# Two constants of the scheduler's cost table, set while a two-layer hybrid trunk is built

## The chip, the cores and the metric

The kernel runs on one core of one Trainium2 chip. The metric is the time of one execution on the device in microseconds (us), taken from before the first instruction to after the last. The core has a matrix engine (TensorE, PE in the rows), a vector engine (VectorE, DVE), a scalar engine (ScalarE, ACT), GpSimd (POOL), a queue that issues the transfers (SyncE, SP) and 16 DMA engines. Each engine works through its own list of instructions in the order in which the program has them, and waits on semaphores for the others.

## What is computed

Two layers of a decoder trunk for 512 positions and a width of 1024, batch 1. Each layer normalises its input, projects it once, sends the pieces through three causal mixers (A: a state-space block in chunks, "SSD"; B: a diagonal complex scan, "S5"; C: attention with low-rank queries and keys, "MLA"), gates and sums the three, and projects back:

```python
for l in range(DEPTH):                       # DEPTH = 2
    h = rms_norm(x, pre_norm[l])
    proj = h @ w_in[l]
    z_a, xbc, dt_raw, u_b, z_b, c_q, c_kv, k_rope, z_c, gate_logits = split_columns(proj)
    y_a = ssd_branch(z_a, xbc, dt_raw, ...) @ w_a[l]
    y_b = s5_branch(u_b, z_b, ...) @ w_b[l]
    y_c = mla_branch(c_q, c_kv, k_rope, z_c, ...) @ w_c[l]
    gates = sigmoid(gate_logits).reshape(bsz, s, N_BRANCH, D_MODEL)
    merged = gates[..., 0, :] * y_a + gates[..., 1, :] * y_b + gates[..., 2, :] * y_c
    out = merged @ w_o[l]
    x = x + rms_norm(out, post_norm[l])
```

## The kernel before

Everything is float32. TensorE multiplies in a rounded float32, so each operand is split into a high part and the rest, and a product is made of three matmuls: high by high, high by low, low by high. `mm3` (L61, L62, L63) does that for small products. `dense` does it for a block of 128 output rows by 512 positions with 1024 inputs: sixteen matmuls with the high weights (L116 and L117, by turns with the activation's high and low part), then eight with the low weights (L119).

A weight block comes through `weight`: one transfer of 512 KB on SP's queue into `wf` (L102; L100 where the block is gathered from eight pieces in DRAM), a cast on ScalarE into `wh` (L66), and a subtraction on VectorE or GpSimd into `wl` (L78, L81). Each of the three tiles has two buffers, so a load waits until the block two before has been split. The results stand in PSUM: three banks `mm` for dense blocks, three banks `aux` for small products, and the two tags `pM` and `pb` (tiles `pM`, `pm`, `pk`, `pr`).

One layer goes through these stages (times of the first layer; the second repeats them some 980 us later):

- 0 to 50 us: normalising, and the first two projections.
- 50 to 380 us: attention (`mla`) for four groups of heads, and between its steps, by `fill`, the pieces of `s5_prep`, which build the S5 filters: transposes into `pm` (L377), `pmh` and `pml` split from it, small products `pM` (L386, L387) and `pk` (L395), and results stored in DRAM as `kpad` and `odr`.
- 380 to 490 us: the S5 scan over 63 steps (`s5_scan`, L896 to L899, four small VectorE operations a step on the tile `ms`, 252 in all), beside the eight merges of branch C on TensorE.
- 490 to 690 us: SSD. Convolutions on VectorE (`keep`, L69) behind dense projections; for each of four groups the product `aux` of the split tiles `bfh`, `bfl` and `cfh`, `cfl` (L61 to L63), and small products after it.
- 690 to 840 us: eight S5 blocks (`s5_block`): each loads `uf`, `sf`, `kpad` (eight pieces of 64 KB) and `odr`, splits them, and multiplies (`pM`); its result `ys` is transposed into an `aux` bank (L936). Each block stands beside a dense projection and a merge of branch A.
- 840 to 1030 us: the GLU, the merges of branch B, and the output projection.

The order of each engine's list is not written by hand. The program is recorded step by step, and while it is recorded a scheduler inside `tile.TileContext(nc, schedule_with_timeline_sim=True)` (L1228) puts the instructions in order: it plays the program through with a table of costs and, at each point of its own clock, takes for each engine an instruction whose inputs it holds to be ready. Buffers are handed out in the order of the program's text, so the dependencies are the same whatever the order. Two entries of the table matter here: the gap that it adds to every matmul at full clock (2.5 ns), and the delay between the end of a transfer and the moment at which a waiting engine sees it (900 ns).

The names in the rows and orders are those of the tiles; a number behind a name is the buffer.

## Time and profile before

| | us |
|---|---|
| time, median of 3 runs | 1972.35 (1971.62 to 1976.9) |
| profiled execution | 1977.92 |
| its span, first to last instruction | 1976.1 |
| TensorE busy | 1870.3 (95%) |
| VectorE busy | 1420.3 (72%) |
| ScalarE busy | 914.2 (46%) |
| GpSimd busy | 631.9 (32%) |
| TensorE's granted clock, mean | 0.967 of full speed |

The profile is of one execution. Its own time lies 1.8 us above its span, and 5.6 us above the median of the runs; a difference is worked out within it and then put on the median. Busy time of an engine counts an instruction from its start to its end. Matmuls overlap, so TensorE counts as busy from the start of one to the end of the next. An idle time stands in brackets behind the instruction that ended it, with the one that released it.

### The profile page before, as it was taken

Reading aid. Unit: us, or ns where it says so; the run is one execution under the profiler, and the core shown is the slowest. Engines: PE = TensorE matmul, PEld = TensorE weight load, DVE = VectorE, ACT = ScalarE, POOL = GpSimd, SP = SyncE. Lnnn points to the kernel's source line nnn. Section 1 sums busy time; section 2 is a strip of 40 time slices with the busy share of each in tenths; the row PEclk is TensorE's granted clock in tenths of the full one; section 3 lists DMA queues with packets and bytes.
Section 4 is the critical chain, followed back from the end, with each engine's and each line's share of the span. In section 5 each row is a group of like instructions: output and inputs, shape, how many; then the busy total and the mean of one; then the engine's idle time right before and its main releaser. Section 6 shows DMA issues by size and latency. Waiting matters only on the chain.

```text
span 1976.1 us, 28153 instructions
## 1 busy us (share of the span) xinstructions
PE 1870.3 (95%) x9880; PEld 1528.1 (77%) x9880; DVE 1420.3 (72%) x2882; ACT 914.2 (46%) x1647; POOL 631.9 (32%) x679
## 2 busy tenths in 40 slices
PE   7898999899999989999998989999999999999998
PEld 5687777687877868888876877776878887788887
DVE  6866566799999857744578566667999996776443
ACT  4355455522555545533332555554235663554331
POOL 1746656201233201201118465661013331012010
PEclk9898998899999999999997999998999999999999
DMA  5343333322321266345233334343332224662541
GB/s 158 94 114 94 108 114 103 119 92 84 128 65 64 75 187 182 92 152 167 90 83 90 111 93 122 100 128 96 96 130 75 74 76 113 183 174 86 171 128 43
DMA packets 136253, 219.99 MB, mean 111 GB/s; under 512 B 39856, under 2 KB 79408, under 8 KB 135600
## 3 DMA queue, kind: packets, MB, share of 16 engines
q1 hardware_dynamic: 136112, 218.19, 37.1%
q8 instruction: 78, 1.28, 0.3%
q14 instruction: 63, 0.52, 0.1%
HBM read 182.08 MB, written 31.33 MB: 108 GB/s over the span
## 4 chain that ended last, share of the span: by engine, by line
PE 60%; DVE 22%; DMA 9%; ACT 3%; issue 2%; POOL 2%; SPq 2%; DVEq 0%; ACTq 0%; POOLq 0%
PE mm L116 15%; PE mm L117 14%; PE mm L119 14%; DMA wf<-in_w_in 3%; DVE wl L78 3%; DVE keep L69 3%; PE mm L61 2%; PE mm L62 2%; PE mm L63 2%; PE aux L61 1%; DVE tmp L69 1%; DVE ms L899 1%; PE aux L62 1%; PE aux L63 1%; DVE sc_t L896 1%
## 5 line engine op out<-in xcount | busy, mean ns | idle before, releaser
L116 PE MATMUL mm<-hh,wh 128*128 128x512 f32 (+1 forms) x1232 | 499.5, 405 | 11.5 <-ACT wh L66 8.0
L66 ACT ACTIVATE wh<-wf 128x1024 fp32r<-128x1024 f32 (+1 forms) x294 | 291.3, 994 | 440.2 <-PE mm L117 227.2
L117 PE MATMUL mm<-hl,wh 128*128 128x512 f32 (+1 forms) x1232 | 492.0, 399 | 0.0
L78 DVE TENSOR_TENSOR wl<-wf,wh 128x1024 fp32r<-128x1024 f32 (+1 forms) x243 | 294.8, 1218 | 188.1 <-ACT wh L66 154.3
L119 PE MATMUL mm<-hh,wl 128*128 128x512 f32 (+1 forms) x1232 | 314.9, 393 | 1.9 <-DVE wl L78 1.9
L116 PEld LDWEIGHTS mm<-hh,wh 128*128 128x128 f32 (+1 forms) x1232 | 236.5, 192 | 72.2 <-ACT wh L66 11.6
L117 PEld LDWEIGHTS mm<-hl,wh 128*128 128x128 f32 (+1 forms) x1232 | 236.2, 192 | 48.5 <-issue 0.5
L119 PEld LDWEIGHTS mm<-hh,wl 128*128 128x128 f32 (+1 forms) x1232 | 228.2, 188 | 52.6 <-DVE wl L78 2.3
L81 POOL TENSOR_TENSOR mg<-mg,tmp 128x512 f32<-128x512 f32 x32 | 77.7, 2431 | 458.1 <-DVE tmp L78 240.5
L81 POOL TENSOR_TENSOR wl<-wf,wh 128x1024 fp32r<-128x1024 f32 (+1 forms) x51 | 108.9, 2135 | 302.6 <-PE mm L119 209.3
L116 PE MATMUL mm<-ah,wh 128*128 128x512 f32 x512 | 200.3, 393 | 0.0
L117 PE MATMUL mm<-al,wh 128*128 128x512 f32 x512 | 199.9, 391 | 0.0
L119 PE MATMUL mm<-ah,wl 128*128 128x512 f32 x512 | 127.6, 390 | 0.0
L116 PEld LDWEIGHTS mm<-ah,wh 128*128 128x128 f32 x512 | 96.2, 188 | 21.4 <-ACT pkf L66 0.7
L117 PEld LDWEIGHTS mm<-al,wh 128*128 128x128 f32 x512 | 96.1, 188 | 20.9 <-issue 1.0
L119 PEld LDWEIGHTS mm<-ah,wl 128*128 128x128 f32 x512 | 95.7, 188 | 19.6
L617 DVE CUSTOM_DVE_ANT_0 sc<-aux,cmask 128x128 f32<-128x128 f32 (+3 forms) x128 | 60.9, 485 | 63.5 <-PE aux L63 62.5
L66 ACT ACTIVATE sc<-sc,nm 128x128 f32<-128x128 f32 (+3 forms) x128 | 70.4, 554 | 13.3 <-DVE nm L73 13.2
L81 POOL TENSOR_TENSOR pv<-pq,ar 128x288 f32<-128x288 f32 x64 | 49.1, 789 | 77.2 <-PE pk L395 68.7
L69 DVE SCALAR_TENSOR_TENSOR keep<-mm,cw,keep 128x511 f32<-128x511 f32 (+2 forms) x96 | 71.1, 740 | 2.0 <-ACT keep L66 1.5
L66 ACT ACTIVATE tmp<-mm 128x512 f32<-128x512 f32 x76 | 44.8, 592 | 56.2 <-PE mm L63 31.5
L81 POOL TENSOR_TENSOR pw<-pbb,ar 128x256 f32<-128x256 f32 x64 | 51.0, 799 | 41.8 <-PE pm L377 41.6
(346 smaller groups left out, 4002.8 us busy)
## 6 DMA issues: line engine op xcount, KB each, us to landing
wf<-in_w_in SPq DMA_DIRECT2D x156, 512.0 KB, 3.6
odr<-pv SPq DMA_DIRECT2D x64, 128.0 KB, 2.0
wf<-in_w_c SPq DMA_DIRECT2D x16, 512.0 KB, 3.4
wf<-in_w_a SPq DMA_DIRECT2D x16, 512.0 KB
wf<-kpad SPq DMA_DIRECT2D x128, 64.0 KB, 6.4
wf<-odr SPq DMA_DIRECT2D x16, 512.0 KB, 7.1
wf<-in_w_glu SPq DMA_DIRECT2D x16, 512.0 KB, 3.4
wf<-in_w_b SPq DMA_DIRECT2D x16, 512.0 KB, 3.8
```

What stands on the lines that cost most here:

```text
L61: mm(out, ah, bh, start=start, stop=False)
L62: mm(out, ah, bl, start=False, stop=False)
L63: mm(out, al, bh, start=False, stop=stop)
L66: self.nc.scalar.activation(out, in_, func, **kw)
L69: self.nc.vector.scalar_tensor_tensor(out, in0, s, in1, op0, op1)
L78: self.nc.vector.tensor_tensor(out, a, b, op)
L81: self.nc.gpsimd.tensor_tensor(out, a, b, op)
L116: mm(ps[:m], wh[:, o(i)], bh, start=i == 0, stop=False)
L117: mm(ps[:m], wh[:, o(i)], bl, start=False, stop=False)
L119: mm(ps[:m], wl[:, o(i)], bh, start=False, stop=i == k - 1)
L617: nc.vector.tensor_tensor_reduce(out=sc, in0=ps[:, :n], in1=self.cmask[:, 512 - n:512], op0=ALU.add, op1=ALU.max, scale=1.0, scalar=-3.0e3 ...
L896: nc.vector.tensor_tensor(t1, sc1, s, ALU.mult)
```

## The change

The function `measured_costs` sets two entries of the scheduler's cost table while the program is built, and puts the old values back afterwards. The gap of a matmul at full clock goes from 2.5 ns to 13.6 ns, the delay behind a transfer from 900 ns to 1600 ns. The text of the trunk is the same.

```diff
@@ -1,4 +1,4 @@
-from contextlib import ExitStack
+from contextlib import ExitStack, contextmanager
 
 import numpy as np
 
@@ -1214,6 +1214,22 @@
     return d
 
 
+@contextmanager
+def measured_costs():
+
+    from concourse.hw_specs import TRN2Spec
+
+    costs = {"PE_FULL_CLOCK_PASS_GAP_NS": 13.6, "SEM_PROP_DMA_OVERHEAD_NS": 1600}
+    saved = {k: getattr(TRN2Spec, k) for k in costs}
+    for k, v in costs.items():
+        setattr(TRN2Spec, k, v)
+    try:
+        yield
+    finally:
+        for k, v in saved.items():
+            setattr(TRN2Spec, k, v)
+
+
 def kernel(**inputs):
     import concourse.bacc as bacc
     from concourse.bass_utils import run_bass_kernel_spmd
@@ -1225,7 +1241,7 @@
         for n, v in arrays.items()
     }
     out = nc.dram_tensor("out_0", (T, D), F32, kind="ExternalOutput").ap()
-    with tile.TileContext(nc, schedule_with_timeline_sim=True) as tc:
+    with measured_costs(), tile.TileContext(nc, schedule_with_timeline_sim=True) as tc:
         trunk(tc, aps, out)
     r = run_bass_kernel_spmd(nc, [{f"in_{n}": v for n, v in arrays.items()}], core_ids=[0])
     return r.results[0]["out_0"].reshape(1, T, D)
```

The two programs hold the same instructions on every engine, 9714 on TensorE, 2874 on VectorE, 1489 on ScalarE, 684 on GpSimd and 1041 on SP, with the same buffers. What differs is the order of each list. It is the same from 0 to 50 us, through most of 745 to 1000 us, from 1400 to 1440 us and from 1725 us to the end. It differs in the attention stages, at the end of each scan, in SSD, and in the first S5 blocks. Three places follow; a line with - is where an instruction stood, one with + where it stands now.

**Place A**, the end of the scan in layer one. First VectorE's list around `wl_5309`, the low weights of a projection, and `keep_5260`, a convolution; `ms_4355` and `sc_t` belong to the scan.

```order
 L69 SCALAR_TENSOR_TENSOR keep_5221<-tmp_5226,keep_5221 128x512
 L78 TENSOR_TENSOR wl_5309<-wf_5307,wh_5308 128x1024
-L898 TENSOR_TENSOR ms_4355<-ms_4355,sc_t1_4357 128x64
 L69 SCALAR_TENSOR_TENSOR keep_5260<-mm_5235,cw_5177,keep_5260 128x511
-L899 TENSOR_TENSOR ms_4355<-ms_4355,sc_t2_4358 128x64
 L69 SCALAR_TENSOR_TENSOR keep_5260<-mm_5235,cw_5177,keep_5260 128x510
-L896 TENSOR_TENSOR sc_t1_4357<-sc1_0_560,ms_4355 128x64
-L897 TENSOR_TENSOR sc_t2_4358<-sc2_0_561,ms_4355 128x64
 L69 SCALAR_TENSOR_TENSOR keep_5260<-mm_5235,cw_5177,keep_5260 128x509
```

The scan's operations that stood among these stand ahead of them now: 238 of the 252 stood ahead of `wl_5309`, now all 252. Ahead of the last step of `keep_5260` it is 252 in place of 246.

TensorE's list behind this: `mm_5375` is a dense projection, `aux_5354` the first product of SSD, of the tiles `cf` (split from `keep_5260`) and `bf` (split from `keep_5221`).

```order
 L117 MATMUL mm_5375<-hl_111,wh_5370 128x512
 L116 MATMUL mm_5375<-hh_110,wh_5370 128x512
+L61 MATMUL aux_5354<-cfh_5348,bfh_5346 128x128
 L117 MATMUL mm_5375<-hl_111,wh_5370 128x512
 L116 MATMUL mm_5375<-hh_110,wh_5370 128x512
 L117 MATMUL mm_5375<-hl_111,wh_5370 128x512
+L62 MATMUL aux_5354<-cfl_5349,bfh_5346 128x128
+L63 MATMUL aux_5354<-cfh_5348,bfl_5347 128x128
```

The twelve matmuls of `aux_5354` stood 45 dense matmuls later; VectorE's `cfl_5349`, which they read, has moved forward as well, past the last convolution steps of `keep_5299`, those of `keep_5338`, and a block of low weights. In layer two the same place has 244 scan operations ahead of `wl_15093` where 232 stood.

**Place B**, the third and fourth S5 block of layer one. ScalarE's list: `wh_7650` and `wh_7851` are cast from the `odr` of two blocks, a block apart, `wh_7742` and `wh_7792` from dense weights, `ys` and `gl` belong to the blocks' results.

```order
 L66 ACTIVATE wh_7650<-wf_7649 128x1024
-L66 ACTIVATE wh_7792<-wf_7791 128x1024
-L66 ACTIVATE tmp_7739<-mm_7714 128x512
+L66 ACTIVATE wh_7742<-wf_7741 128x1024
+L66 ACTIVATE keep_7621<-mm_7596 128x512
 L66 ACTIVATE gl_7583<-aux_7574 128x512
 L66 ACTIVATE ys_7655<-pM_7656 64x4x8x16
@@ -608,9 +605,11 @@
 L66 ACTIVATE ys_7655<-pM_7657 64x4x8x16
 L66 ACTIVATE wh_7851<-wf_7850 128x1024
+L66 ACTIVATE wh_7792<-wf_7791 128x1024
```

The cast `wh_7792` stood behind `wh_7650` and stands behind `wh_7851`; `wh_7742` and `wh_7709` ahead of it have also moved back by a block. On SP's queue the loads of these weights have moved behind the pieces of `kpad` and the `odr` of their block, which they stood ahead of.

TensorE's list in the same place: `mm_7714` and `mm_7747` are dense blocks, `pM_7656` is the product of the third S5 block, and `wh_7637` is split from its `kpad`.

```order
 L116 MATMUL mm_7714<-hh_110,wh_7709 128x512
 L117 MATMUL mm_7714<-hl_111,wh_7709 128x512
-L119 MATMUL mm_7714<-hh_110,wl_7710 128x512 x8
-L116 MATMUL mm_7747<-ah_5755,wh_7742 128x512
-L117 MATMUL mm_7747<-al_5756,wh_7742 128x512
-L116 MATMUL mm_7747<-ah_5808,wh_7742 128x512
-L117 MATMUL mm_7747<-al_5809,wh_7742 128x512
-L116 MATMUL mm_7747<-ah_6224,wh_7742 128x512
-L117 MATMUL mm_7747<-al_6225,wh_7742 128x512
 L61 MATMUL pM_7656<-wh_7637,uh_7626 64x128
```

The eight matmuls with `wl_7710` and six of `mm_7747` that stood ahead of `pM_7656` have gone behind it, and four more follow. Further on, the transposes `aux_7775` of the block's result have moved ahead of the sixteen matmuls of `mm_7797` with `wh_7792`. In SSD the product of each of the three later groups (`aux_5821`, `aux_6290`, `aux_6759`, as `aux_5354` above) has likewise moved ahead of some ten dense matmuls, and its `cfl` on VectorE past one operation.

**Place C**, early in the attention stage of layer two, VectorE's list: `cql` and `ckl` are low parts of the normalised latents (`keep_10410`, `keep_10488`, `keep_10489`), `pu2` and `pml` belong to `s5_prep`.

```order
 L78 TENSOR_TENSOR tmp_10681<-krdt_10211,cosT_234 32x512
+L78 TENSOR_TENSOR pu2_11025<-puf_10627,pu2_11025 128x8x64
+L78 TENSOR_TENSOR cql_10576<-keep_10410,cqh_10575 128x512
 L78 TENSOR_TENSOR tmp_10680<-tmp_10680,sinT_236 32x512
+L69 SCALAR_TENSOR_TENSOR keep_10488<-keep_10488,kvn_10220,aux_10666 128x512
+L69 SCALAR_TENSOR_TENSOR keep_10489<-keep_10489,kvn_10220,aux_10666 128x512
+L78 TENSOR_TENSOR pml_11136<-pm_11132,pmh_11135 128x256
 L78 TENSOR_TENSOR tmp_10681<-tmp_10681,tmp_10680 32x512
+L78 TENSOR_TENSOR ckl_10669<-keep_10488,ckh_10668 128x512
 L78 TENSOR_TENSOR ql_10749<-mm_10735,qh_10748 64x512
 L519 STREAM_SHUFFLE tmp_10775<-mm_10762 128x512
```

The operations on `keep_10488`, `keep_10489` and `pml_11136` have moved forward past operations of the attention (`ql_10749`, `tmp_10776`, `wl_10840` among them), and `pu2_11025` has moved back behind some that stood after it.

## Rows read from the trace of the kernel before

**Rows 1.** Page: busy time of the engines, shares of the last chain:

```profile
PE 1870.3 (95%) x9880; PEld 1528.1 (77%) x9880; DVE 1420.3 (72%) x2882; ACT 914.2 (46%) x1647; POOL 631.9 (32%) x679
PE 60%; DVE 22%; DMA 9%; ACT 3%; issue 2%; POOL 2%; SPq 2%; DVEq 0%; ACTq 0%; POOLq 0%
```

**Rows 2.** Stages: stretch, length, busy us (instructions) by engine, clock, DMA:

```profile
50.00:380.00 330.00, 298.80 (x1607) 243.84 (x1606) 222.19 (x492) 171.23 (x393) 197.90 (x265) 0.93 0.36 104
490.00:690.00 200.00, 196.25 (x1064) 160.08 (x1063) 183.54 (x299) 109.18 (x179) 61.94 (x43) 0.98 0.26 82
690.00:745.00 55.00, 47.84 (x343) 38.51 (x342) 33.95 (x41) 26.26 (x37) 5.69 (x3) 1.00 0.67 176
745.00:1030.00 285.00, 282.29 (x1477) 233.82 (x1476) 168.00 (x258) 119.99 (x177) 41.25 (x25) 1.00 0.43 130
1030.00:1355.00 325.00, 295.62 (x1591) 241.68 (x1589) 222.75 (x495) 168.22 (x388) 202.80 (x265) 0.93 0.37 105
1490.00:1660.00 170.00, 170.00 (x959) 140.04 (x958) 161.24 (x267) 97.11 (x160) 54.91 (x39) 1.00 0.23 74
```

**Rows 3.** Timeline of PE at full clock (start, us, engine, line, operation):

```profile
1880.37 1.98 PE L119 MATMUL mm<-hh,wl 128*128 128x512 f32 x8
1882.18 0.39 PE L116 MATMUL mm<-ah,wh 128*128 128x512 f32 x1
703.81 0.22 PE L61 MATMUL pM<-wh,sh 128*64 128x128 f32 x1
703.87 0.22 PE L62 MATMUL pM<-wl,sh 128*64 128x128 f32 x1
```

**Rows 4.** Waits of PE: who waited for whom, us in total, times, longest:

```profile
PE pm L377 <- ACT pkf L66: 9.9, 4, 3.7
PE pM L387 <- DVE pml L78: 5.3, 4, 4.2
```

**Rows 5.** Timeline of DVE, then PE, at the end of the first scan:

```profile
454.71 0.28 DVE L896 TENSOR_TENSOR sc_t<-sc,ms 128x64 f32<-128x64 f32 x1
455.73 0.28 DVE L896 TENSOR_TENSOR sc_t<-sc,ms 128x64 f32<-128x64 f32 x1
489.79 0.69 DVE L69 SCALAR_TENSOR_TENSOR keep<-tmp,keep 128x512 f32<-128x512 f32 x1
...
486.23 2.11 PE L119 MATMUL mm<-hh,wl 128*128 128x512 f32 x8 [1.92 <-DVE wl L78]
490.48 0.40 PE L116 MATMUL mm<-hh,wh 128*128 128x512 f32 x1
```

**Rows 6.** Timeline of PE in the SSD part of the first layer:

```profile
593.86 0.33 PE L62 MATMUL aux<-cfl,bfh 128*128 128x128 f32 x1 [1.24 <-DVE cfl L78]
641.41 0.33 PE L62 MATMUL aux<-cfl,bfh 128*128 128x128 f32 x1 [0.79 <-DVE cfl L78]
```

**Rows 7.** Timeline of PE, then ACT, in the first S5 blocks:

```profile
708.26 0.50 PE L116 MATMUL mm<-hh,wh 128*128 128x512 f32 x1 [3.00 <-ACT wh L66]
726.85 0.27 PE L61 MATMUL pM<-wh,uh 128*64 128x128 f32 x1 [1.31 <-ACT wh L66]
740.66 0.70 PE L936 MATMUL aux<-ident,ys 64*128 64x64 f32 x8 [0.84 <-ACT ys L66]
743.25 0.22 PE L61 MATMUL pM<-wh,uh 128*64 128x128 f32 x1
...
725.75 1.06 ACT L66 ACTIVATE wh<-wf 128x1024 fp32r<-128x1024 f32 x1 [4.81 <-DMA wf<-kpad]
740.51 2.95 ACT L66 ACTIVATE wh<-wf 128x1024 fp32r<-128x1024 f32 x3
```

**Rows 8.** Timeline of PE early in the attention part of layer two:

```profile
1079.39 0.42 PE L387 MATMUL pM<-pu,pml 128*128 128x64 f32 x1 [4.22 <-DVE pml L78]
```

**Rows 9.** Stretches behind two waits, columns as in rows 2:

```profile
594.00:602.00 8.00, 8.00 (x30) 6.85 (x30) 7.27 (x11) 3.64 (x6) 2.93 (x3) 0.57 0.19 66
1062.00:1073.00 11.00, 9.56 (x25) 7.30 (x26) 9.78 (x16) 3.68 (x7) 10.55 (x15) 0.54 0.45 137
```

## The prediction

> **What bounds the kernel now.** Read the page's busy times first: TensorE is busy for 1870.3 of 1976.1 us, and the chain that ended last runs through it for 60% and through VectorE for 22% [rows 1]. A reordering can't shorten a matmul; it can only give back, or add, time in which TensorE stands still. So read the stages next [rows 2]. The long dense stretch from 745 to 1030 us leaves 2.71 us idle (285.00 less 282.29): nothing is to be had there. The two attention stages leave 31.20 and 29.38 us (330.00 less 298.80, 325.00 less 295.62), at a mean clock of 0.93, with no other engine above 70%: there TensorE waits for single operations that stand late in another engine's list. SSD leaves 3.75 us in layer one and nothing in layer two, with VectorE busy for 183.54 of 200 and 161.24 of 170 us: there two engines run side by side with little slack. The first S5 blocks leave 7.16 of 55 us with the DMA engines at 0.67. So the change can win in attention, where waits are many and engines free, and can lose at the end of the scan and in SSD, where an operation that is moved forward pushes another back.
>
> [...]
>
> [...]
>
> **Place A and SSD.** All steps of the scan now stand ahead of `wl_5309`; before, 14 of the 252 operations stood behind it. A round of four takes 1.02 us (455.73 less 454.71) [rows 5], so `wl_5309` starts 14/4 times 1.02, 3.6 us later. TensorE already waited 1.92 us for it at 486.23 [rows 5], so nothing covers this: +3.6 us. The next wait is no second cost. `aux_5354` stands at about 490.48 in TensorE's old time, 494.1 with the 3.6. The last step of `keep_5260` ended at 490.48 (489.79 and 0.69) and has 6 more scan operations ahead, 1.5 us: 492.0. Its cast on ScalarE goes beside two VectorE operations, and the subtraction `cfl_5349` after them; three times about 0.65, as that last step takes, makes 493.9. So it is just ready. If ScalarE's cast is late, the wait comes on top, at most the 3 us that a cast behind five others of such a size would take.
>
> In layer two 12 more scan operations stand ahead of `wl_15093`, 3 times 1.02, 3.1 us; its wait did not show before, so part is slack. In SSD that follows, layer two has no idle time to give back [rows 2]; layer one has 3.75 us at most. On the other hand TensorE's products of the three later groups have moved ahead of ten dense matmuls (2.3 us) and their `cfl` past only one operation of some 0.7 us: the waits of 1.24 and 0.79 us at 593.86 and 641.41 [rows 6] grow by about 1.6 us each. These are not added to the 3.6: VectorE does the same work in sum and is not late after the scan, so a wait for it takes in what TensorE had lost before. I take +3.6 for layer one, scan and SSD together (bounds +1.6, one such wait, and +8.4, the 3.6 and three of them), and +3 for layer two (0 to +6). Sum +6.6.
>
> **Place B.** Here an S5 block's `wh` is cast as soon as its `kpad` lands: ScalarE stood idle 4.81 us for one at 725.75 [rows 7]. The order can't bring that forward, but it has moved TensorE's product `pM_7656`, which needs it, ahead of 18 dense matmuls, 14 of which ran before it: 14 times 226 ns are 3.2 us less cover, so the wait of 1.31 us at 726.85 [rows 7] grows to 4.5. Those 14 then run after it and fill the next wait; alone this would cost little. But the fill ends at `mm_7797`. Its weights `wh_7792` are now cast behind `wh_7851`, which is the first of three casts that took 2.95 us from 740.51 [rows 7]; the second of them ended two thirds through, at 742.5, and that place is now that of `wh_7792`. `aux_7775`, now ahead of it, ran at 740.66. So the sixteen matmuls and the eight after them, which ended at 743.25, would end 24 times 226 ns, 5.4 us, after 742.5: at 747.9, 4.7 us late. Against this stands that the chain of `kpad` loads starts up to 1.3 us earlier, by the wait that goes, and that the 3.00 us at 708.26 [rows 7] can shrink where TensorE comes late already. Bounds 0 and +4.7 a layer; I take 2.5, about the middle, twice: +5. That SP's loads of dense weights have moved behind `kpad` and `odr` is part of this price and not counted again.
>
> **Place C and the rest of attention.** The largest wait of the trace is 4.22 us at 1079.39, for `pml`, which stood late in VectorE's list [rows 8]; the new order has it ahead of five operations, and the wait goes. But `ckl` and `pu2` share that list, and the dense product and `pM` that need them stand next on TensorE: I count half as won, -2. Waits for `pkf` (9.9 us in 4) and `pml` (5.3 us in 4) [rows 4] are the ones that the order touches; at other places of the stage it moves operations both ways, and I take -2 for all of them. Sum -4; bounds -15.2, if all of both go, and +6, if as much is made anew at as many places as are improved.
>
> **The clock.** Behind a wait the granted clock can fall to its lower level: 0.57 in the mean over the 8 us from 594, behind the 1.24 us at 593.86, and 0.54 over 11 us from 1062 [rows 9]. The first costs (1 less 0.57) times 8, 3.4 us. Not each wait does it: behind the 1.92 us at 486.23 the clock stayed up. For the new waits at A and B against those that go at C I add a third of one such stretch, +1 (bounds -4 and +7).
>
> **Sum.** 6.6 and 5, less 4, and 1: +8.6 us on the profiled execution, whose span is 1976.1 and whose own time is 1977.92. It is 5.6 us above the median of the runs; I put the difference on the median: 1972.35 and 8.6, **1981 us**.
>
> **The rivals.** (1) *Faster: the attention waits decide.* The place is the list of VectorE and ScalarE in the two attention stages. If the waits for `pkf` and `pml` all go, 15.2 us [rows 4] are won, and the stretch of low clock from 1062 or its like, with 9.56 busy us at about half speed [rows 9], gives back up to 5. Less the 11.6 lost at A and B that is -8.6: 1964 us. For it: 60 us of idle time lie there and the engines are free. Against it: only one of the eight waits is seen to go in the order, and new ones appear beside it. It decides once the attention stages win more than 11.6 us together. (2) *No difference.* SSD takes in the loss at the scan's end, since VectorE leads there, and the S5 blocks only exchange the 3.00 us at 708.26 for longer waits at `kpad`. Then A leaves 1.6 twice, B nothing, C -4: 1972 us. For it: the same work, small moves, and long stretches that are word for word the same. (3) *Much slower: the clock.* Every new wait at A, B and in SSD brings a low stretch of 3.4 us: with four of them 13.6 in place of the 1, 1994 us. Against it: the clock is 1.00 from 690 to 745 in spite of 7 us of idle time [rows 2]. (4) *The change does nothing*, because the table is read before it is set: excluded, the lists of all engines differ.
>
> **How the numbers follow.** About 0.3%, 5.9 us, is what a measurement of this kernel can tell from no change, so the bounds lie at 1966.4 and 1978.3. The forecast, between 1978.3 and 1988, has 0.32; rival 1 0.29; rival 2 0.28; rival 3 0.11; rival 4 none. The forecast and rival 3 are slower. The range leaves out the far half of rival 3 and the farthest part of rival 1: 1958 to 1996. Faster 0.29, same 0.28, slower 0.43.
>
> **What would show it.** For A: TensorE's wait at `wl_5309` above 5 us, near 490, and 194 us or less busy of the 200 in SSD. For B: the wait for `wh` of `kpad` near 727 at 4 us or more, and one of 4 us at `aux_7775` or `mm_7797` near 740. For C: no wait of 4 us near 1079, and a shorter one for `ckh` or `pu2` there. The forecast is wrong if the idle time of the attention stages falls by over 10 us, or if TensorE's wait for `wl_5309` stays near 2.

## The result, and the profile after

The changed kernel takes 2005.69 us, the median of 4 runs (2004.27 to 2006.9). The kernel before, run beside it, took 1974.62 (4 runs, 1971.62 to 1981.42). The ratio is 1.0138, with an interval of 1.0119 to 1.0158: 27 us slower. The forecast was 1981, its range ended at 1996. The direction was right, the size was not.

The profiled execution took 2006.81 us. From its page: the span, the busy time of the engines, and the shares of the last chain, as in [rows 1].

```profile
span 2004.9 us, 28118 instructions
PE 1876.0 (94%) x9880; PEld 1533.9 (77%) x9880; DVE 1434.9 (72%) x2882; ACT 910.1 (45%) x1647; POOL 632.3 (32%) x679
PE 45%; DVE 32%; DMA 10%; issue 4%; ACT 4%; POOL 2%; SPq 1%; DVEq 0%; ACTq 0%; POOLq 0%
```

Three things are to be seen against [rows 1]. TensorE's idle time goes from 105.8 us (1976.1 less 1870.3) to 128.9 (2004.9 less 1876.0): 23.1 of the 28.8 us that the span has grown are waits. VectorE's share of the last chain goes from 22% to 32%. And VectorE is busy for 14.6 us longer, 1434.9 against 1420.3, with the same 2882 instructions. A change of order alone has made instructions last longer. The mean granted clock hardly differs: 0.966, against 0.967.

Five of the stages, with the columns of [rows 2]. Each stretch is cut where about the same work begins and ends: the counts of matmuls agree within 8, some 2 us, so lengths can be compared no closer than that.

```profile
50.00:376.00 326.00, 293.33 (x1606) 240.00 (x1605) 221.57 (x492) 169.28 (x394) 202.07 (x264) 0.94 0.37 105
493.00:698.00 205.00, 196.21 (x1062) 160.19 (x1061) 183.99 (x288) 105.07 (x174) 61.52 (x43) 0.99 0.24 72
698.00:752.00 54.00, 48.08 (x335) 39.22 (x335) 36.48 (x43) 26.55 (x38) 5.69 (x3) 0.94 0.66 176
1038.00:1367.00 329.00, 297.67 (x1595) 244.10 (x1594) 221.10 (x496) 168.19 (x389) 203.55 (x264) 0.93 0.35 104
1504.00:1686.00 182.00, 175.15 (x960) 142.91 (x959) 169.53 (x271) 95.77 (x160) 54.23 (x39) 0.98 0.22 70
```

The first attention stage is 4 us shorter than its 330 before, the second 4 us longer than its 325: together no gain. SSD of layer one is 5 us longer. The last row is SSD of layer two. There TensorE had not stood still at all (170.00 of 170.00); now it is idle for 6.85 us (182.00 less 175.15), and the stretch takes 12 us more for 960 matmuls in place of 959. The granted clock in it is 0.98 where it was 1.00, by estimate some 3.6 of the 12 us (0.02 times 182). VectorE is busy for 169.53 of the 182 us. What this stretch costs by itself, a run below says.

The two traces can also be compared at the same amount of work, by the columns that TensorE has multiplied. By that measure the changed kernel is 1.1 us early at 425 us of the old time, and late by 5.1 us at 690, 6.8 at 780, 9.2 at 1425, 14.8 at 1495 and 26.9 at 1725. So the trace puts most of the loss at the scan's end and in SSD of both layers, 12.1 us of it in SSD of layer two.

### The profile page after: what moved, and what is told of

Same layout as the page of the kernel before. It is cut to its first block, busy times and chain, and to the rows that moved or that the text cites. A ratio compares the mean times of both kernels' runs of the same rounds, so it can differ in the third digit from the quotient of the medians.

```text
span 2004.9 us, 28118 instructions
## 1 busy us (share of the span) xinstructions
PE 1876.0 (94%) x9880; PEld 1533.9 (77%) x9880; DVE 1434.9 (72%) x2882; ACT 910.1 (45%) x1647; POOL 632.3 (32%) x679
## 4 chain that ended last, share of the span: by engine, by line
PE 45%; DVE 32%; DMA 10%; issue 4%; ACT 4%; POOL 2%; SPq 1%; DVEq 0%; ACTq 0%; POOLq 0%
PE mm L116 10%; PE mm L117 10%; PE mm L119 10%; DVE wl L78 5%; DVE keep L69 4%; DMA wf<-in_w_in 4%; PE mm L61 2%; PE mm L62 2%; PE mm L63 2%; DVE ms L899 2%; DVE tmp L78 2%; DVE sc_t L896 1%; DVE tmp L69 1%; DVE ms L898 1%; ACT wh L66 1%
## 5 line engine op out<-in xcount | busy, mean ns | idle before, releaser
L119 PE MATMUL mm<-hh,wl 128*128 128x512 f32 (+1 forms) x1232 | 320.6, 396 | 5.6 <-DVE wl L78 4.1
L66 ACT ACTIVATE tmp<-keep 128x512 f32<-128x512 f32 x48 | 30.2, 630 | 87.5 <-DVE keep L69 82.7
```

Of the source, the lines that this page charges most:

```text
L66: self.nc.scalar.activation(out, in_, func, **kw)
L119: mm(ps[:m], wl[:, o(i)], bh, start=False, stop=i == k - 1)
```

## The experiments

**How the parts were separated.** A program built with the transfer delay alone has the lists of the kernel before, word for word; one built with the gap alone has those of the changed kernel. So only the gap acts, and what is to be tried apart is the order. Most of the following kernels are the kernel before with each engine's list fixed by order edges, taken from the old order outside one stretch and from the new one inside it:

```diff
+def keep_order(tc, nc):
...
+    for packed in ORDER.values():
...
+        for x, y in zip(names, names[1:]):
+            tc.add_manual_dep(traced[y], x, info, reason="order")
...
         trunk(tc, aps, out)
+        keep_order(tc, nc)
```

With the old lists throughout, this yields the program of before. What each run then shows as its diff is a move out of its lists. Differences in us are the recorded ratio less 1, times the median of before in that session (1976.99, 1978.57 and 1977.19 us). The quotient of the two medians differs from that ratio by up to 0.002.

**Four stretches.** SSD of layer two alone (1495 to 1675 us), here ScalarE's list:

```diff
-L66 ACTIVATE wh_16180<-wf_16179 128x1024
 L66 ACTIVATE tmp_15968<-tmp_15968 128x512
 L66 ACTIVATE sth_15874<-stf_15876 128x256
+L66 ACTIVATE wh_16180<-wf_16179 128x1024
```

> All lists are those of the kernel before, but from 1495 to 1675 us (SSD of layer two) they are those of the change. Theory 1 (in SSD VectorE has no slack, and the new lists put other VectorE operations beside GpSimd's, which then last longer): the loss of 11 to 12 us that the changed kernel shows in this stretch appears alone, 1984 to 1988 us against 1974.6, with VectorE busy some 10 us longer there. Theory 2 (the stretch is slow because it is entered late, after the loss at the scan's end): within 4 us of before, 1972 to 1978.

Measured: 1985.84 us, ratio 1.0047 (1.003 to 1.0063), +9.3 us.

The scan's end in layer two alone (1425 to 1495 us), here VectorE's list; the eight scan operations ahead of the weights stood behind them before:

```diff
+L896 TENSOR_TENSOR sc_t1_14180<-sc1_1_10383,ms_14178 128x64
+L897 TENSOR_TENSOR sc_t2_14181<-sc2_1_10384,ms_14178 128x64
 L78 TENSOR_TENSOR wl_14795<-wf_14793,wh_14794 128x1024
```

> Only from 1425 to 1495 us (end of the scan of layer two, first convolutions) the lists are those of the change. Theory 1: the 5.5 us that the changed kernel loses there appear, 1978 to 1982 us, and SSD behind it, in its old order, adds nothing. Theory 2: SSD, entered 5 us late, loses 11 more: 1988 to 1994. The step of the prediction (scan ahead of low weights): +3, 1977 to 1978.

Measured: 1980.3, ratio 1.0016 (1.0002 to 1.003), +3.2 us.

Layer one from the scan's end through the first S5 blocks (425 to 780 us), places A and B in one:

```diff
 L66 ACTIVATE wh_7851<-wf_7850 128x1024
+L66 ACTIVATE wh_7792<-wf_7791 128x1024
```

> Only from 425 to 780 us (end of the scan, SSD and first S5 blocks of layer one) the lists are those of the change. By the two traces the changed kernel loses 8 us there (from 1.1 us early to 6.8 us late): 1981 to 1984. The prediction's steps gave 6: 3.6 for scan and SSD and 2.5 for the S5 blocks. If the stretches hang together across the cuts, less: 1975 to 1979.

Measured: 1988.3, ratio 1.0053 (1.0031 to 1.0074), +10.5 us.

Both attention stages (0 to 425 and 1000 to 1425 us), place C among them:

```diff
+L78 TENSOR_TENSOR pml_11136<-pm_11132,pmh_11135 128x256
...
+L78 TENSOR_TENSOR ckl_10669<-keep_10488,ckh_10668 128x512
```

> From 0 to 425 and from 1000 to 1425 us (attention of both layers, with the start of the merges) the lists are those of the change, elsewhere those of before. By the two traces the changed kernel is level there (-0.2 and +1 us): 1973 to 1977. The prediction had -4, 1970; its first rival -15, 1960.

Measured: 1980.75, ratio 1.0011 (0.9998 to 1.0023), +2.2 us, which is not told from no change; its ten runs lie between 1973.12 and 1982.63, and the profiled one is the fastest of them.

The four add up to 25.2 of the 27 us. So the loss lies in the SSD part of layer two, in layer one behind the attention, and at the scan's end of layer two; no gain in attention shows.

**Layer one, in three.** The scan's end (425 to 534 us), SSD (534 to 690) and the S5 blocks (690 to 780), one each:

```diff
+L61 MATMUL aux_5354<-cfh_5348,bfh_5346 128x128
 L117 MATMUL mm_5375<-hl_111,wh_5370 128x512
```

> Only from 425 to 534 us (end of the scan of layer one and the first SSD products) the lists are those of the change. The prediction's step: 14 scan operations more ahead of the low weights, +3.6, given back at most by waits that stand there already: 1979 to 1982 us against 1978. Rival (VectorE is not late in sum, so SSD takes it in): within 2 us.

Measured: 1981.51, ratio 1.0022 (1.0005 to 1.0039), +4.3 us.

```diff
+L61 MATMUL aux_5764<-mmh_5685,xdh_5403 64x128
+L61 MATMUL aux_5778<-mmh_5698,xdh_5403 64x128
```

> Only from 534 to 690 us (SSD of layer one from its second group on) the lists are those of the change. Theory 1, as in layer two (VectorE beside GpSimd; its operations are 4 us longer in this stretch of the changed kernel): +4 to +7, 1982 to 1985. If layer two's loss is peculiar to it: within 2 us.

Measured: 1979.34, ratio 1.001 (0.9993 to 1.0027), +2 us, not told from no change.

```diff
-L66 ACTIVATE wh_7792<-wf_7791 128x1024
...
 L66 ACTIVATE wh_7851<-wf_7850 128x1024
+L66 ACTIVATE wh_7792<-wf_7791 128x1024
```

> Only from 690 to 780 us (first S5 blocks of layer one) the lists are those of the change. The prediction's step: +2.5 (0 to 4.7), 1978 to 1983. By the trace of the kernel with the lists of the change from 425 to 780 us the stretch gives nothing: late by 8.0 us at its start and at its end: 1976 to 1979.

Measured: 1980.06, ratio 1.0014 (0.9995 to 1.0033), +2.8 us, not told from no change either. The three make 9.1 of the 10.5 us. Of these only the scan's end is shown by itself (1.0 to 7.7 us).

**What SSD of layer two lost.** In the new kernel TensorE waits there for VectorE's results and nothing else. The waits of TensorE from 1515 to 1695 us (us in total, times, longest); the same view of the kernel before, from 1495 to 1675, is empty:

```profile
PE aux L63 <- DVE stl L78: 2.7, 2, 1.7
PE aux L62 <- DVE cfl L78: 2.6, 2, 1.4
PE aux L61 <- DVE er L78: 1.3, 2, 1.0
PE mm L116 <- DVE keep L69: 0.4, 1, 0.4
```

These waits come to 7.0 us; the lower clock of the stretch, 0.98, comes on top. VectorE is late because some of its operations last longer. Groups of instructions by form in the stretch from 1400 to 1750 us (count, then busy us, mean ns, and what ended the idle time before them), first of the kernel before:

```profile
L69 DVE SCALAR_TENSOR_TENSOR keep<-tmp,keep 128x512 f32<-128x512 f32 x16 | 14.3, 891 | 3.5 <-ACT tmp L66 3.5
L78 DVE TENSOR_TENSOR tmp<-tmp,cbm 128x512 f32<-128x512 f32 x16 | 11.0, 715 | 0.5 <-ACT tmp L66 0.5
L73 DVE TENSOR_SCALAR tmp<-tmp,sn 128x512 f32<-128x512 f32 x8 | 9.0, 1131 | 1.0 <-ACT tmp L66 0.7
```

and of the changed kernel:

```profile
L69 DVE SCALAR_TENSOR_TENSOR keep<-tmp,keep 128x512 f32<-128x512 f32 x16 | 18.2, 1137 | 3.6 <-ACT tmp L66 3.6
L78 DVE TENSOR_TENSOR tmp<-tmp,cbm 128x512 f32<-128x512 f32 x16 | 17.1, 1072 | 0.5 <-ACT tmp L66 0.4
L73 DVE TENSOR_SCALAR tmp<-tmp,sn 128x512 f32<-128x512 f32 x8 | 11.2, 1400 | 1.7 <-ACT tmp L66 1.4
```

The same sixteen products `tmp<-tmp,cbm` take 6.1 us more, the other two groups 3.9 and 2.2 more; a fourth group, `stl`, takes 5.0 us in place of 7.0. Which of the sixteen, and beside what, the timeline shows (start, us, engine, line, operation, idle before). One place in the kernel before: ScalarE, GpSimd, then VectorE.

```profile
1551.06 1.06 ACT L66 ACTIVATE wh<-wf 128x1024 fp32r<-128x1024 f32 x1 [1.07 <-PE mm L117]
1552.58 0.63 ACT L66 ACTIVATE tmp<-tmp 128x512 f32<-128x512 f32 x1 [0.45 <-DVE tmp L75]
...
1553.00 2.40 POOL L81 TENSOR_TENSOR wl<-wf,wh 128x1024 fp32r<-128x1024 f32 x1 [1.67 <-ACT wh L66]
...
1553.06 0.85 DVE L75 TENSOR_SCALAR tmp<-pr,cs 128x128 f32<-128x128 f32 x3
1553.94 0.75 DVE L69 SCALAR_TENSOR_TENSOR tmp<-keep,dsk,aux 64x512 f32<-64x512 f32 x1
1554.71 1.23 DVE L78 TENSOR_TENSOR tmp<-tmp,cbm 128x512 f32<-128x512 f32 x1
```

The same place in the changed kernel:

```profile
1570.68 0.63 ACT L66 ACTIVATE tmp<-tmp 128x512 f32<-128x512 f32 x1 [3.72 <-DVE tmp L75]
1571.22 0.40 ACT L66 ACTIVATE sth<-stf 128x256 fp32r<-128x256 f32 x1
1571.52 1.04 ACT L66 ACTIVATE wh<-wf 128x1024 fp32r<-128x1024 f32 x1
...
1572.64 2.38 POOL L81 TENSOR_TENSOR wl<-wf,wh 128x1024 fp32r<-128x1024 f32 x1 [3.21 <-ACT wh L66]
...
1572.04 0.75 DVE L69 SCALAR_TENSOR_TENSOR tmp<-keep,dsk,aux 64x512 f32<-64x512 f32 x1
1572.82 2.75 DVE L78 TENSOR_TENSOR tmp<-tmp,cbm 128x512 f32<-128x512 f32 x1
1575.83 0.68 DVE L78 TENSOR_TENSOR tmp<-tmp,cbm 128x512 f32<-128x512 f32 x1
```

GpSimd computes one block of low weights, 2.4 us in both. Before, ScalarE's cast `wh` stood ahead of `tmp` and `sth`, so GpSimd began 1.71 us before VectorE's first product (1554.71 less 1553.00). VectorE did in that time what reads a PSUM tile, `pr` and `aux` (the latter in 0.75 us, as in the changed kernel, where GpSimd overlaps it by 0.15 us); the product then took 1.23 us in place of 0.68. Now the cast stands behind `tmp` and `sth`, GpSimd begins 0.18 us before the product, and the product lasts 2.75 us: it ends at 1575.57, 0.55 us after GpSimd (1572.64 and 2.38, 1575.02). Before it ended 0.54 us after GpSimd too. The same stands in three of the four groups of SSD: 2.77, 2.75 and 2.76 us, at 1525.17, 1572.82 and 1620.30. The other thirteen products take 0.67 to 0.69 us. This is what a reader must know of the view: the delay is in no wait and in no bracket; it is in the length of the instruction.

So the trace has the product at 2.75 us in place of 0.68 beside GpSimd's subtraction, and the read of PSUM beside the same subtraction at 0.75 us (1553.94), against 0.74 where GpSimd is idle (1547.21 of `short_before`, a run below). By the profile GpSimd need not have started first: `tmp<-tmp,sn` at 1542.36 us of the changed kernel starts 0.04 us ahead of GpSimd's sum `ssq<-ssq,tmp` (1542.40, 1.29 us), and still takes 1.62 us in place of 0.49 (1536.35, where GpSimd is idle) and ends 0.29 us after it. What holds VectorE up in such a place, no trace shows.

**Whose list it is.** In the same stretch, only VectorE's and ScalarE's lists of the changed kernel, then only TensorE's. The first holds the move of `wh_16180` above; the second has moves such as

```diff
-L61 MATMUL aux_15601<-mmh_15521,xdh_15226 64x128
 L62 MATMUL aux_15587<-mml_15509,xdh_15226 64x128
 L63 MATMUL aux_15587<-mmh_15508,xdl_15227 64x128
+L61 MATMUL aux_15601<-mmh_15521,xdh_15226 64x128
```

> From 1495 to 1675 us (SSD of layer two) only VectorE's and ScalarE's lists are those of the change; TensorE's and all else are those of before. Theory 1 (the casts moved on ScalarE and the operations moved on VectorE put VectorE's work beside GpSimd's): nearly all of the 9 us of the stretch appear, 1983 to 1987 us against 1977, with VectorE's operations 6 to 7 us longer in sum. Theory 3 (TensorE's products of SSD, moved ahead of dense matmuls, wait for VectorE, as the prediction had it): 3 us or less.

> From 1495 to 1675 us only TensorE's list is that of the change. Theory 1: VectorE's operations keep their durations, so at most 3 us: 1975 to 1980. Theory 3: 6 to 9 us, 1983 to 1986, with waits of TensorE for cf, er and st of 1 to 2 us each, nine in all.

Measured: 1990.83 with VectorE's and ScalarE's lists, ratio 1.0054 (1.0034 to 1.0074), +10.7 us, all that `ssd2` has; 1983.55 with TensorE's, ratio 1.0012 (0.9994 to 1.003), +2.4 us, not told from no change, with up to 5.9 us left open. The sixteen products in the two, first of VectorE's and ScalarE's lists:

```profile
L78 DVE TENSOR_TENSOR tmp<-tmp,cbm 128x512 f32<-128x512 f32 x16 | 17.1, 1075 | 0.5 <-ACT tmp L66 0.4
```

and with TensorE's list alone:

```profile
L78 DVE TENSOR_TENSOR tmp<-tmp,cbm 128x512 f32<-128x512 f32 x16 | 12.0, 779 | 0.5 <-ACT tmp L66 0.5
```

So the lists that feed GpSimd and VectorE are enough for the whole loss, without TensorE's products moved forward, on which the prediction looked. What TensorE's list costs by itself stays unclear: in its trace the sixteen products take 12.0 us, where before has 11.0. ScalarE's list alone was not tried.

**Taking the cause away.** GpSimd's subtraction is cut to an eighth for the weights of SSD in layer two (the first of them are split while the scan still runs, from 1442 us on), once with the old lists and once with those of `ssd2`:

```diff
+        pool_lo = self.lo_pool and self.nw % self.lo_pool == 0
+        self.short = pool_lo and self.lo8
+        n = 128 if self.short else n
...
-            mm(ps[:m], wl[:, o(i)], bh, start=False, stop=i == k - 1)
+            mm(ps[:m], (wh if short and i else wl)[:, o(i)], bh, start=False, stop=i == k - 1)
```

> All lists are those of before, but in SSD of layer two GpSimd subtracts the low weights of its blocks for one eighth of the columns only (0.4 us in place of 2.4 each); TensorE multiplies by the high weights again in the place of the rest, so that its work stays. This is left out of the result. Theory 1: VectorE's operations are stretched less, 2 to 6 us faster than before, 1971 to 1975. If GpSimd's length doesn't matter to VectorE: 1977.

> The same shortened low weights on GpSimd (seven eighths of them left out), with the lists of the change from 1495 to 1675 us. Theory 1: with GpSimd's long operations gone, the new lists lose only 2 to 4 us against the old ones with the same shortening, not 9: 1974 to 1979. Theory 3, or any cause in the lists alone: still 8 to 10 us more than the other shortened kernel.

Measured: 1975.09 with the old lists, ratio 0.9976 (0.9966 to 0.9986); 1975.5 with the new ones, 0.9989 (0.9973 to 1.0006). The two orders now lie 2.6 us apart by the ratios (0.9989 less 0.9976, times 1978.57) and 0.4 by the medians, where they lay 9.3 apart. Groups of 1400 to 1750 us, with the old lists:

```profile
L78 DVE TENSOR_TENSOR tmp<-tmp,cbm 128x512 f32<-128x512 f32 x16 | 10.6, 687 | 3.1 <-ACT tmp L66 2.9
L73 DVE TENSOR_SCALAR tmp<-tmp,sn 128x512 f32<-128x512 f32 x8 | 9.0, 1128 | 1.6 <-ACT tmp L66 1.6
L81 POOL TENSOR_TENSOR wl<-wf,wh 128x128 fp32r<-128x128 f32 x13 | 6.7, 519 | 149.5 <-ACT wh L66 149.5
```

and with those of `ssd2`:

```profile
L78 DVE TENSOR_TENSOR tmp<-tmp,cbm 128x512 f32<-128x512 f32 x16 | 11.3, 712 | 0.6 <-ACT tmp L66 0.4
L73 DVE TENSOR_SCALAR tmp<-tmp,sn 128x512 f32<-128x512 f32 x8 | 11.2, 1406 | 1.6 <-ACT tmp L66 1.4
```

The products are down to 712 ns in spite of the new order. What is left, 2.2 us in `tmp<-tmp,sn`, is as much as in the changed kernel (1400 ns in the mean). There seven of the eight take 1.14 to 1.62 us, each beside one of GpSimd's sums `ssq<-ssq,tmp` (1.27 to 1.54 us), and the eighth takes 0.49; the sums were not cut. The 2.2 us are near the 2.6, but the intervals of the two ratios overlap. The edit also spares TensorE seven of eight products with GpSimd's result; none of its waits in the stretch was for that result. So the clash with GpSimd is the cause in SSD of layer two; this is shown and not only argued.

**A gap half way.** The scheduler builds with a gap of 6.7 ns, about half of 13.6, and with the delay left at 900:

```diff
-    costs = {"PE_FULL_CLOCK_PASS_GAP_NS": 13.6, "SEM_PROP_DMA_OVERHEAD_NS": 1600}
+    costs = {"PE_FULL_CLOCK_PASS_GAP_NS": 6.7}
```

> [...] If a longer gap as such is to blame (the planner then holds TensorE to be slower than VectorE), about half the loss: 1985 to 1992 us. If it is a matter of which operations happen to meet GpSimd's, anything from 1970 to 2005.

Measured: 1987.99, ratio 1.0061 (1.0041 to 1.008), +12 us. Its sixteen products take 798 ns in the mean, nearer to before's 715 than to 1072, and yet it is slower than before. By the work done, its trace is 3.9 us late at 425 us, 7.2 at 690, 8.3 at 1495 and 7.7 at 1725: it loses mostly before 690 us, in the first attention stage and behind it, and nothing in SSD of layer two. So the clash in that stretch explains nothing of its 12 us, and what does is open. The time lies in both expected ranges, so this run does not decide between them: that a longer gap as such makes the order slower is not excluded, with 12 us for 6.7 ns and 27 for 13.6.

## Why the prediction was right and wrong

**Place A came out in size, by luck.** It had 3.6 us for layer one and 3 for layer two; the runs give 4.3 (`scan1`, 1.0 to 7.7) and 3.2 (`scan2`, 0.4 to 5.9). TensorE in the changed kernel:

```profile
465.46 1.52 PE L119 MATMUL mm<-hh,wl 128*128 128x512 f32 x6
473.43 2.11 PE L119 MATMUL mm<-hh,wl 128*128 128x512 f32 x8 [1.53 <-DVE wl L78]
483.12 0.47 PE L116 MATMUL mm<-hh,wh 128*128 128x512 f32 x1 [2.15 <-DVE keep L69]
488.46 2.02 PE L119 MATMUL mm<-hh,wl 128*128 128x512 f32 x8
```

The six matmuls at 465.46 stood at 466.55 before, those of `wl_5309` at 486.23 [rows 5]: 1.1 us early has become 2.2 us late, a loss of 3.3. It does not come at `wl_5309`, as the prediction said, but at two earlier places, at the weights ahead of it and at a convolution. The scan's steps were moved ahead of those too. The sum was right, the wait that carries it was not: "above 5 us, near 490" is not there, and the wait of 1.92 us is gone. VectorE and GpSimd at `wl_5309`, before and then in the changed kernel:

```profile
482.79 3.39 DVE L78 TENSOR_TENSOR wl<-wf,wh 128x1024 fp32r<-128x1024 f32 x1
482.68 2.42 POOL L81 TENSOR_TENSOR wl<-wf,wh 128x1024 fp32r<-128x1024 f32 x1 [10.82 <-ACT wh L66]
...
484.35 1.22 DVE L78 TENSOR_TENSOR wl<-wf,wh 128x1024 fp32r<-128x1024 f32 x1
485.39 2.40 POOL L81 TENSOR_TENSOR wl<-wf,wh 128x1024 fp32r<-128x1024 f32 x1 [14.56 <-ACT wh L66]
```

Before, the subtraction itself met GpSimd's and took 3.39 us. Now it starts 1.56 us later, as the scan's steps are ahead of it, but 1.04 us before GpSimd, takes 1.22 us and ends 0.61 us sooner. So the wait to which the prediction added 14 steps was made by the clash that it did not know, and went with it. No run separates the clash from the steps at the scan's end.

**The SSD step failed.** "VectorE does the same work in sum and is not late after the scan, so a wait for it takes in what TensorE had lost before" reckoned VectorE's work as a fixed number of us. It is fixed in instructions only. In layer two they last longer beside GpSimd (the products 1072 ns in the mean in place of 715), TensorE waits 7.0 us for VectorE, and the +3 for scan and SSD together became 3.2 and 9.3. This is the step that failed. In layer one the same products do not last longer. The sixteen of 420 to 760 us, before and after:

```profile
L78 DVE TENSOR_TENSOR tmp<-tmp,cbm 128x512 f32<-128x512 f32 x16 | 10.8, 683 | 0.1
L78 DVE TENSOR_TENSOR tmp<-tmp,cbm 128x512 f32<-128x512 f32 x16 | 10.8, 688 | 0.4 <-ACT tmp L66 0.2
```

Yet in the changed kernel that stage is 5 us longer, with no more work for VectorE (183.99 us busy against 183.54 in [rows 2]). In the trace of `ssd1`, where the scan is the old one, TensorE's waits from 530 to 690 us are 8.8 us in place of 3.5, all but 0.8 of them for VectorE, and the 3.00 us at 708.26 [rows 7] are down to 1.02. So the moved products do wait there, and a later wait takes part of it in, as the prediction had it; that run as a whole is +2 us and unclear.

**Place B was not borne out.** The forecast had 2.5 us a layer. The run by itself has 2.8, too near to zero to be told. In the changed kernel the waits that it named do not show: the third block's product stands at 729.33 without a wait for `wh`, and near 740 the longest is 1.19 us, at 744.38. There is one of 1.79 us for `wh` a block earlier, at 715.54. What the run by itself does have is a lower clock, 0.94 where [rows 2] has 1.00, in the same stretch of `s5_1`:

```profile
690.00:745.00 55.00, 45.88 (x299) 36.64 (x298) 33.16 (x42) 25.06 (x36) 3.64 (x3) 0.94 0.64 165
```

In the changed kernel the clock is 0.94 as well, and the stage takes 54 us, but with 8 matmuls fewer in the cut than before; by the work done it loses 1.7 us from 690 to 780 (5.1 us late, then 6.8). In layer two it loses nothing (26.9 us late at 1675 and at 1725). That TensorE comes late already, and finds the weights there, would explain this; no run shows it.

**Attention was taken too high.** The waits that were to go have mostly gone: `pkf` from 9.9 to 2.8 us and `pml` from 5.3 to 0.8 [rows 4]. Others have come in their place. Four kinds of waits of TensorE, over the whole of the kernel before:

```profile
PE aux L61 <- DVE mx L617: 7.8, 11, 1.7
PE aux L237 <- DVE tmp L73: 5.3, 2, 3.4
PE aux L649 <- DVE pl L78: 2.8, 5, 1.1
PE aux L61 <- DMA qh<-rrh: 3.4, 1, 3.4
```

and after:

```profile
PE aux L61 <- DVE mx L617: 11.5, 7, 4.0
PE aux L237 <- DVE tmp L73: 8.3, 4, 4.0
PE aux L649 <- DVE pl L78: 5.9, 6, 2.6
PE aux L61 <- DMA qh<-rrh: 6.1, 2, 3.5
PE pm L377 <- ACT pkf L66: 2.8, 3, 1.4
PE pM L387 <- DVE pml L78: 0.8, 2, 0.4
```

The first four grow from 19.3 to 31.8 us, by 12.5, about what `pkf` and `pml` gave back (15.2 less 3.6, 11.6). The step "I take -2 for all of them" had no ground but the list of waits that would end. The 4.22 us of place C [rows 8] went, as forecast. It was not "the largest wait of the trace": that is one of 9.2 us at the kernel's start (L434, for `tmp`), outside the attention.

**The clock and the rivals.** By estimate from its mean, the granted clock took 65.2 us before (0.033 times 1976.1) and 68.2 after (0.034 times 2004.9), 3 us more, so the term of +1 (bounds -4 and +7) held, and rival 3, with 13.6, is not what happened. The rivals named attention, an exchange of waits and the clock; none was a VectorE that gets slower by what runs beside it, and without the 9.3 us of that the measured time would lie near the range's end at 1996. Set out by terms: the scan's ends 6.6 forecast (with SSD in it) and 7.5 measured, SSD 0 of its own and 9.3 in layer two (with the unclear 2 of layer one, 11.3), S5 of both layers 5 and an unclear 2.8 in the one that was run, attention -4 and an unclear 2.2.

The 226 ns that the prediction takes for a dense matmul are the distance of eight of them in [rows 3] (1882.18 less 1880.37, by 8). How much of it is a gap, no run shows, so which of the two constants is nearer to the chip is open. What the runs show is the order: with the longer gap it is the slower one.

## What to carry to other kernels

Other constants in the planner's table do not make a better order by themselves; here they made one that is 27 us slower. It set a VectorE product just behind the start of a GpSimd operation three times, at 2 us each (2.75 to 2.77 us in place of 0.68), and the other table that was tried lost 12 us in other places. Before a reordering is priced, look at which operations will run beside each other on VectorE and GpSimd, above all where VectorE is busy for nine tenths of a stretch (161.24 of 170 us here, in SSD of layer two). And compare the mean duration of one form of instruction between two traces, as well as the waits: a change that moves only the order need not change it, and where it does, look at what ran beside it.

## What the hardware showed that was not expected

In three places of the changed kernel a VectorE product, `tmp<-tmp,cbm`, that takes 0.68 us elsewhere took 2.75 to 2.77 us. There it began 0.17 or 0.18 us after GpSimd had begun on 128x1024 elements, and it ended 0.54 or 0.55 us after GpSimd. `tmp<-tmp,sn`, with one SBUF tensor and a scalar, is lengthened too: 1.60 to 1.62 us in five places beside GpSimd's sum, against 0.49 in one without it (1400 ns in the mean of the eight, 1131 before). The read of PSUM at 1553.94 us of the kernel before, beside GpSimd's subtraction, was not (0.75 us, against 0.74 with GpSimd idle in `short_before`).

Cutting GpSimd's share of these weights to an eighth makes even the old order 4.7 us faster (0.9976). That gain is not in SSD of layer two, where TensorE never waited before: in the trace of `short_before` the same matmul is 5.3 us early at 1495 us and 5.2 at 1680. What goes is a wait of 1.75 us at 1462.29, at the scan's end: there a scan step, `ms` at 1458.89, took 1.81 us in place of 0.28 beside GpSimd's block of weights (1458.06, 2.51 us). So the kernel before paid for the same clash, in that place; the rest of the 4.7 us is not located.
